# Output projection by token halves, with four weights kept in the large slots, and the second half's residual affine moved into the down projection

## The chip, the cores and the metric

The kernel runs on one core of a Trainium2 chip. The engines named below are TensorE (PE, with its weight loads, PEld), VectorE (DVE), ScalarE (ACT), GpSimd (POOL) and SyncE (SP), whose queue issues the DMA transfers. Each engine works through its own queue in order. The metric is the device time of one execution in microseconds (us).

## The reference

One layer of a diffusion backbone over 1024 tokens of width 1024. The attention part runs unchanged here; what matters begins with the output projection `w_out`, the first layer norm, and the convolutional feed-forward network.

```python
    y = (g_a * (o_a @ w_branch_a) + g_b * (o_b @ w_branch_b)) @ w_out
    x = _layer_norm(DEEPNORM_ALPHA * x + gate1 * y, ln1_g[l], ln1_b[l])
    h = x * (1.0 + scale2) + shift2
    y = _conv_ffn(h, w_up[l], conv_w[l], conv_b[l], w_down[l])
    x = _layer_norm(DEEPNORM_ALPHA * x + gate2 * y, ln2_g[l], ln2_b[l])

def _conv_ffn(h, w_up, conv_w, conv_b, w_down):
    u = h @ w_up                      # 1024 -> 5632
    u = depthwise_conv3_over_tokens(u, conv_w) + conv_b
    gate, val = jnp.split(u, 2, axis=-1)
    return (jax.nn.silu(gate) * val) @ w_down
```

Everything is float32. The kernel splits each operand into a high part that TensorE multiplies exactly and a low rest, so each product takes three matmuls (`mm3`: high by high, low by high, high by low).

## The kernel before

Features lie on the 128 partitions, so an activation of 1024 features is eight tiles, f = 0 to 7, of 128 x 1024 tokens. The stages that matter are, in the order in which PE meets them:

- `y`, the output projection. `wout_start(f)` loads the weights of the 128 output features of f, splits them (high part `hwo` by ACT, low part `lwo` by DVE) and loads the residual `x` into `z`; `wout_z` adds the gated product to `z` and gathers the sums `zs` and squares `zq` for the norm. Features 0 to 3 are computed for all 1024 tokens; then 4 to 7 for the token slices `LN1_S`: 0 to 511, 512 to 767 and 768 to 1023.
- LN1, made by `ln_steps` once for each slice: statistics by small matmuls (`sta`), the two diagonals (`dgr`, `dgm`), their broadcast over the partitions (`bcr`, `bcm`), and eight `apply` steps, which normalise a tile of `z` and call `emit1`. `emit1` makes `zo`, the affine value for the later residual (by POOL for odd f, by ACT for even f), and stores it in `zd`; makes the high part of the feed-forward input `B` and the modulated value over `z` itself (two ACT rows); and subtracts them for the low part of `B` (POOL for even f, DVE for odd f).
- `u`, three direct up tiles (two of gate, one of value, in slices; then three more at full width), whose operand is `B`.
- `up_tile` for j = 3 to 21: the up projection by a scheme of seven products instead of eight, into the banks a, b, c, d. Besides `B` it needs the operands `T13` and `T24`, sums of quarters of the modulated value, which `build` makes from `z` in four steps for each k = 0 to 3.
- The down projection: `ya`, first token half, 22 blocks j of 24 matmuls each, which need the weights `hwd`, `lwd` and the gated activation `g` (loaded back from `gd`); during block 6 the stored residuals are loaded from `zd` into the `zz` tiles. Then the second half, `yl`, and LN2.

From `y` on the order of PE's work is that of the code (`manual_schedule`); on the other engines a scheduler places the instructions. LN1 and `build` steps wait in the list `pend`. `tick` counts matmul columns, divided by 0.8, and releases the next step when the count reaches its number, so `LN1_F`, `LN1_D` and `BLD` place the steps between matmuls. Tiles come from pools: `ht` is a pool of large slots that `hput` gives back; the weights use two rings of four tiles, "w" and "wd".

Of the kernel before, what the change touches and what calls it, by code (L numbers as in the profile page):

```python
# [67 lines left out]
def layer_kernel(  # L68
# [773 lines left out]
    def weight(src, nm, n=8, tag="w", he=None, le=None, rtag="raw"):  # L842
        if rtag:
            r = post.tile([P, 8, P], F32, tag=rtag, name=f"r{nm}", bufs=3)[:, 0:n]
        else:
            r = ht(f"r{nm}", (P, n, P))
            hput(f"r{nm}")
        nc.sync.dma_start(r, src)
        pool = wq if tag == "w" else post
        h = pool.tile([P, 8, P], R32, tag=tag, name=f"h{nm}", bufs=4)[:, 0:n]  # L850
        l = pool.tile([P, 8, P], R32, tag=tag, name=f"l{nm}", bufs=4)[:, 0:n]
        split(r, h, l, he or nc.gpsimd, le or nc.gpsimd)
        return h, l
# [67 lines left out]
    def tiny(name):  # L921
        return post.tile([P, 8], F32, tag="tiny", name=name, bufs=6)
# [42 lines left out]
    def ln_steps(zs, zq, s, nm, emit, first, gap, gap1, gap2, each, pm=2, order=range(KT)):  # L965
        w = s.stop - s.start
        n = w // P
        mv, m2, rs, mr = (tiny(f"{a}{nm}") for a in ("mv", "m2", "rs", "mr"))
        bcs = []

        def stats():
            ln_flush()
            st = sml(f"st{nm}")
            for t in range(n):
# [32 lines left out]
    zs, zq = tm("zs1"), tm("zq1")  # L1007
    def wout_z(f, s, ps):
# [4 lines left out]
    for f in range(SPLIT_F):  # L1013
        if f > 1:
            wout_start(f)
        ps = big(f"y{f}")
        gemm(ps, wts[f], mrg, 8)
        for hf in (0, 1):
            wout_z(f, hsl(hf), ps[:, hsl(hf)])
    for f in range(SPLIT_F, KT):  # L1020
        wout_start(f)
    tp = {}

    def affine(o, f, src):
        nc.scalar.activation(o, src, AF.Identity, bias=lnx[:, 8 + f:9 + f], scale=lnx[:, f:f + 1])

    def sub(e, o, a, b, op=ALU.subtract):
        e.tensor_tensor(out=o, in0=a, in1=b, op=op)  # L1028

    def emit1(f, s):  # L1030
        hf = s.start // HALF
        w = s.stop - s.start
        c = slice(s.start - hf * HALF, s.stop - hf * HALF)
        if c.start == 0:
            tp["B", f, hf] = ht(f"B{f}_{hf}", (P, 2, HALF), R32)
        t = tp["B", f, hf]
        z = zv(f, s)
        o = ht(f"zo{f}_{s.start}", (P, w))
        hput(f"zo{f}_{s.start}")
        if f % 2:  # L1040
            nc.gpsimd.tensor_scalar(out=o, in0=z, scalar1=lnx[:, 16 + f:17 + f], scalar2=lnx[:, 24 + f:25 + f],
                                    op0=ALU.mult, op1=ALU.add)
        else:
            nc.scalar.activation(o, z, AF.Identity, bias=lnx[:, 24 + f:25 + f], scale=lnx[:, 16 + f:17 + f])
        nc.sync.dma_start(zd[f][:, s], o)
        affine(t[:, 0, c], f, z)
        affine(z, f, z)
        sub(nc.vector if f % 2 else nc.gpsimd, t[:, 1, c], z, t[:, 0, c].bitcast(F32))

    def build(k):  # L1050
        (b11, b21), (b12, b22) = [[zt_[k, hf][:, a] for a in (0, 1)] for hf in (0, 1)]
        st = {}
# [12 lines left out]
        def s2():  # L1065
            st["24"] = t = tm(f"t24_{k}").rearrange("p (a q) -> p a q", a=2)
            sub(nc.vector, t[:, 1], b22, st["13"][:, 1])
            sub(nc.gpsimd if k % 2 else nc.vector, t[:, 0], b21, t[:, 1])
            hput(f"z{k}_0", f"z{k}_1")

# [13 lines left out]

    hput(*[f"m{a}{f}" for f in range(KT) for a in "hl"])
# [12 lines left out]

    gr = {}
    npair = [0]  # L1100

    def gsplit(j, hf, t):
        r = tm(f"rg{j}_{hf}", w=HALF)
        nc.sync.dma_start(r, gd[j][:, hsl(hf)])
        split(r, t[:, 0], t[:, 1], nc.scalar, nc.vector)

    def ring(name, shape, dt=R32):
        pool, tag = ((wq, "w"), (post, "wd"))[npair[0] % 2]
        npair[0] += 1
        return pool.tile(list(shape), dt, tag=tag, name=name, bufs=4)  # L1110

    def wring(src, nm, n=8, le=None):
        r = post.tile([P, 8, P], F32, tag="raw", name=f"r{nm}", bufs=3)[:, 0:n]
        nc.sync.dma_start(r, src)
        h, l = ring(f"h{nm}", (P, 8, P))[:, 0:n], ring(f"l{nm}", (P, 8, P))[:, 0:n]
        split(r, h, l, nc.scalar, le or (nc.gpsimd if npair[0] % 4 else nc.vector))
        return h, l

# [40 lines left out]
    def up_conv(j):  # L1159
# [150 lines left out]
    for j in range(NF):  # L1310
# [3 lines left out]
        for f in range(KT):  # L1314
            mm3(acc[f], (w[0][:, f], w[1][:, f]), (g[:, 0], g[:, 1]), j == 0, j == NF - 1)
        gkeep(j)
        if j == 6:
            lnr = ht("lnr", (P, 2, HALF)), ht("lnr2", (P, 2, HALF))
            for a in (0, 1):
                nc.sync.dma_start(lnr[a], ln2_row[a].partition_broadcast(P))  # L1320
            for k in range(4):
                for hf in (0, 1):
                    zt_[k, hf] = ht(f"zz{k}_{hf}", (P, 2, HALF))
                    for a in (0, 1):
                        nc.sync.dma_start(zt_[k, hf][:, a], zd[k + 4 * a][:, hsl(hf)])

    zs2, zq2 = tm("zs2"), tm("zq2")
    for f in range(KT):
# [204 lines left out]
```

## Time and profile before

| what | value |
|---|---|
| median of three runs | 1653.31 us (1652.52 to 1653.62) |
| the profiled execution | 1654.61 us, its span 1652.8 us |
| mean granted PE clock | 0.985 |
| PE, DVE, POOL, ACT busy | 95%, 70%, 53%, 49% of the span |
| `y` | 830.5 to 923.2 us |
| `u` | 923.2 to 1019.8 us |
| product form of the up tiles | 1019.8 to 1388.6 us |
| `ya` | 1388.6 to 1508.4 us |

All starts are counted from the start of the span. PE is the busiest engine by far, so the profile is read for the stretches in which PE waits, and in these for the engine that it waits for and what that engine was doing.

### The profile page before, as it was taken

What the parts mean: (1) busy time and instruction counts of PE and PEld (TensorE: products, weight loads), DVE (VectorE), ACT (ScalarE), POOL (GpSimd) and SP (SyncE); (2) the same over time, 40 slices, a digit from 0 to 9 for tenths busy, and PEclk for the clock granted to TensorE, in tenths of its full rate; (3) what the DMA queues carried; (4) which work ended last, traced back from release to release, by engine and by line L of the source; (5) the groups of instructions that cost most, each with busy time, mean ns of one, the idle gap of its engine ahead of it and who ended that gap; (6) DMA issues with size and microseconds to landing.
All of it is one profiled execution on the core that took longest, in us unless ns stands there. A gap on an engine that the chain in (4) does not pass through costs nothing. (4 is left out here: it accounts for less than half of the span.)

```text
span 1652.8 us, 22324 instructions
## 1 busy us (share of the span) xinstructions
PE 1569.0 (95%) x7944; PEld 1302.9 (79%) x7944; DVE 1161.6 (70%) x1674; ACT 808.0 (49%) x1462; POOL 876.2 (53%) x781
## 2 busy tenths in 40 slices
PE   7999899999999999999999779999999999999996
PEld 5877788888877887777788667888888888888896
DVE  6899615538887777797644876789899997345535
ACT  4321222458887666787221663444544444433333
POOL 0673202426665555655324663566667773337885
PEclk9999899999999999999999889999999999999998
DMA  9688432322230111011521221122222228653453
GB/s 374 222 307 310 162 103 76 123 74 62 62 99 21 45 33 45 24 27 51 203 77 39 93 86 65 64 79 88 89 78 77 77 93 287 231 195 93 146 173 109
DMA packets 86800, 192.52 MB, mean 116 GB/s; under 512 B 11040, under 2 KB 25888, under 8 KB 86688
## 3 DMA queue, kind: packets, MB, share of 16 engines
q1 hardware_dynamic: 82080, 182.70, 33.3%
q10 hardware_dynamic: 4608, 8.39, 1.4%
q8 instruction: 62, 1.02, 0.3%
q14 instruction: 50, 0.41, 0.1%
HBM read 154.28 MB, written 28.38 MB: 111 GB/s over the span
## 5 line engine op out<-in xcount | busy, mean ns | idle before, releaser
L533 ACT CAST pth<-ptr 128x512 fp32r<-128x512 f32 x188 | 106.1, 591 | 62.4 <-PE ptr L524 59.9
L524 PE MATMUL ptr<-ident,p 128*128 128x128 f32 x816 | 130.0, 278 | 6.6 <-DVE ptl L534 4.6
L534 DVE TENSOR_TENSOR ptl<-ptr,pth 128x512 fp32r<-128x512 f32 x188 | 123.3, 683 | 16.6 <-ACT pth L533 15.6
L420 ACT ACTIVATE p<-p,nm 128x1024 f32<-128x1024 f32 (+2 forms) x128 | 125.4, 983 | 5.4 <-DVE p L453 5.1
L524 PEld LDWEIGHTS ptr<-ident,p 128*128 128x128 f32 x816 | 94.5, 140 | 37.2 <-DVE ptl L534 9.8
L85 POOL TENSOR_TENSOR wlg<-wg,whg 128x512 fp32r<-128x512 f32 x32 | 47.1, 1478 | 118.7 <-ACT whg L80 118.7
L545 PE MATMUL av<-pth,VT 128*128 128x512 f32 x236 | 106.2, 450 | 0.7 <-ACT avs L551 0.3
L546 PE MATMUL av<-ptl,VT 128*128 128x512 f32 x236 | 98.0, 415 | 5.2 <-POOL ptl L85 5.1
L90 PE MATMUL g<-hh,wlg 128*128 128x512 f32 x256 | 99.8, 390 | 0.4 <-POOL wlg L85 0.4
L88 PE MATMUL g<-hh,whg 128*128 128x512 f32 x256 | 100.0, 391 | 0.0
L89 PE MATMUL g<-hl,whg 128*128 128x512 f32 x256 | 99.7, 389 | 0.0
L453 DVE TENSOR_SCALAR_CACHE_REDUCE p<-s,cvt,nmc 128x1024 f32<-128x1024 f32 x64 | 84.4, 1340 | 11.4 <-PE s L409 7.9
L85 POOL TENSOR_TENSOR lwf<-rwf,hwf 128x1024 fp32r<-128x1024 f32 (+1 forms) x36 | 81.7, 2273 | 13.5 <-ACT hwf L80 12.6
L88 PE MATMUL yl<-gr,hwf 128*128 128x256 f32 (+1 forms) x264 | 85.4, 324 | 0.0
L90 PE MATMUL yl<-gr,lwf 128*128 128x256 f32 (+1 forms) x264 | 84.2, 319 | 0.0
L89 PE MATMUL yl<-gr,hwf 128*128 128x256 f32 (+1 forms) x264 | 84.1, 319 | 0.0
L85 POOL TENSOR_TENSOR lwd<-rwd,hwd 128x1024 fp32r<-128x1024 f32 x16 | 38.7, 2421 | 75.0 <-ACT hwd L80 66.1
L408 PE MATMUL s<-KL,q 128*128 128x512 f32 (+2 forms) x192 | 76.6, 399 | 1.7 <-DVE p L453 1.2
L82 POOL TENSOR_SCALAR pth<-prw 128x512 fp32r<-128x512 f32 x48 | 29.8, 620 | 89.5 <-ACT prw L530 85.2
L409 PE MATMUL s<-KL,q 128*128 128x512 f32 (+2 forms) x192 | 71.7, 373 | 0.0
L1233 POOL TENSOR_TENSOR uv<-ve,pe 128x512 f32<-128x512 f32 x19 | 30.4, 1603 | 73.7 <-DVE ve L1233 48.4
L80 ACT CAST wS<-s 128x512 fp32r<-128x512 f32 x76 | 44.6, 621 | 49.4 <-POOL s L1028 37.2
(382 smaller groups left out, 5313.5 us busy)
## 6 DMA issues: line engine op xcount, KB each, us to landing
wml<-in_wmodT_dram SPq DMA_DIRECT2D x48, 512.0 KB
ru<-in_w_up_dram SPq DMA_DIRECT2D x38, 512.0 KB
rwf<-in_w_dnf_dram SPq DMA_DIRECT2D x24, 512.0 KB
rg<-gd SPq DMA_DIRECT2D x44, 256.0 KB
rwd<-in_w_dn_dram SPq DMA_DIRECT2D x22, 512.0 KB
gd<-tg SPq DMA_DIRECT2D x19, 512.0 KB
wm<-in_wmodT_dram SPq DMA_DIRECT2D x16, 512.0 KB
wg<-in_w_g_dram SPq DMA_DIRECT2D x32, 256.0 KB
```

What stands on the lines that cost most here:

```text
L85: lo_eng.tensor_tensor(out=lo, in0=src, in1=hi.bitcast(F32), op=ALU.subtract)
L88: nc.tensor.matmul(ps, a[0], b[0], start=start, stop=False, skip_group_check=resumed)
L89: nc.tensor.matmul(ps, a[0], b[1], start=False, stop=False, skip_group_check=resumed)
L90: nc.tensor.matmul(ps, a[1], b[0], start=False, stop=stop, skip_group_check=resumed)
L408: nc.tensor.matmul(o, self.q[0][:, hs], ks, start=True, stop=False)
L420: nc.scalar.activation(p, s, AF.Exp, bias=nm[:, h:h + 1], scale=scale, accum_out=sm[:, h:h + 1])
L453: nc.vector.tensor_scalar(out=p, in0=o, scalar1=self.qscale(nqs)[:, hs] if self.br else -1.0, scalar2=self.other[:, hs], op0=ALU.mult, op1 ...
L524: nc.tensor.transpose(tr[:, h * P:(h + 1) * P], self.pslice(h, n), ident)
L533: nc.scalar.copy(hi, tr)
L534: nc.vector.tensor_tensor(out=lo, in0=tr, in1=hi.bitcast(F32), op=ALU.subtract)
L545: nc.tensor.matmul(self.av, v, hi, start=first, stop=False)
L546: nc.tensor.matmul(self.av, v, lo, start=False, stop=self.left == 0)
```

## The change

1. `y` is computed two features at a time (`y_pair`): first all eight features for tokens 0 to 511, then all eight for the second half, f = 4 to 7 there in its two slices. LN1 of the first half goes into `pend` before the second half's matmuls begin.
2. To have the weights for both passes, those of f = 0 to 3 (high and low, eight tiles) are kept in large slots of `ht`; 4 and 5 use the ring "w", 6 and 7 the ring "wd". The weights of the first up tile are loaded as soon as 4 and 5 are done, those of the second after `y`.
3. In the second token half `emit1` stores the normalised value as it is, without `zo`. The modulated value, which would overwrite it, goes into new tiles `v`, and `build` reads `v`. The affine left out is done later by `residual`, eight ACT rows of 128x512 on the loaded `zz` tiles, which the code puts into `pend` at block 12 of the down projection; `tick` is called there, and `drain` after it.
4. The additions to `zq` are all on DVE (before, POOL had those of f below 4). `LN1_F`, `LN1_D` have other numbers, `BLD` is 2400 instead of 3600.

PE has as many instructions of each shape as before.

```diff
-SPLIT_F = 4
-LN1_F = 6500.0, 2000.0, 2000.0
-LN1_D = 2500.0, 2000.0, 1000.0, 700.0
+LN1_F = 3500.0, 2000.0, 2000.0
+LN1_D = (2500.0, 2000.0, 2000.0, 2500.0), (2500.0, 2000.0, 1000.0, 700.0), (2500.0, 2000.0, 1000.0, 700.0)
-BLD = 3600.0
+BLD = 2400.0
+ZAJ = 12
+ZAF = 4500.0
...
     def wout_start(f, rtag="raw"):
-        wts[f] = weight(w_out[f], f"wo{f}", 8, tag="w" if f < SPLIT_F + 2 else "wd", he=nc.scalar, le=nc.vector,
-                        rtag=rtag)
+        wts[f] = weight(w_out[f], f"wo{f}", 8, tag=None if f < 4 else "wd" if f & 2 else "w", he=nc.scalar,
+                        le=nc.vector, rtag=rtag)
...
-        ln_add(zv(f, s), zs, zq, s, f == 0, f"a{f}_{s.start}", nc.vector if f >= SPLIT_F else nc.gpsimd, nc.gpsimd)
+        ln_add(zv(f, s), zs, zq, s, first, f"a{f}_{s.start}", nc.vector, nc.gpsimd)
...
+    def residual(o, f, src):
+        nc.scalar.activation(o, src, AF.Identity, bias=lnx[:, 24 + f:25 + f], scale=lnx[:, 16 + f:17 + f])
...
-        o = ht(f"zo{f}_{s.start}", (P, w))
-        hput(f"zo{f}_{s.start}")
-        if f % 2:
-            nc.gpsimd.tensor_scalar(out=o, in0=z, scalar1=lnx[:, 16 + f:17 + f], scalar2=lnx[:, 24 + f:25 + f],
-                                    op0=ALU.mult, op1=ALU.add)
+        v = z
+        if hf:
+            if f < 4 and c.start == 0:
+                tp["v", f] = ht(f"v{f}", (P, 2, HALF))
+            v = tp["v", f % 4][:, f // 4, c]
+            o = z
         else:
-            nc.scalar.activation(o, z, AF.Identity, bias=lnx[:, 24 + f:25 + f], scale=lnx[:, 16 + f:17 + f])
+            o = ht(f"zo{f}", (P, w))
+            hput(f"zo{f}")
+            if f % 2:
+                nc.gpsimd.tensor_scalar(out=o, in0=z, scalar1=lnx[:, 16 + f:17 + f], scalar2=lnx[:, 24 + f:25 + f],
+                                        op0=ALU.mult, op1=ALU.add)
+            else:
+                residual(o, f, z)
         nc.sync.dma_start(zd[f][:, s], o)
         affine(t[:, 0, c], f, z)
-        affine(z, f, z)
-        sub(nc.vector if f % 2 else nc.gpsimd, t[:, 1, c], z, t[:, 0, c].bitcast(F32))
+        affine(v, f, z)
+        sub(nc.vector if f % 2 else nc.gpsimd, t[:, 1, c], v, t[:, 0, c].bitcast(F32))
...
-    for si, s in enumerate(LN1_S):
-        w = s.stop - s.start
-        for f in range(SPLIT_F, KT, 2):
-            ps = big(f"y{f}_{si}")
-            for a in (0, 1):
-                mm_ticked(ps[:, a * HALF:a * HALF + w], wts[f + a], mrg, s)
-            for a in (0, 1):
-                wout_z(f + a, s, ps[:, a * HALF:a * HALF + w])
-        pend += ln_steps(zs, zq, s, f"a{si}", emit1, LN1_F[si], *LN1_D, order=(0, 4, 1, 5, 2, 6, 3, 7))
+    for f in range(0, KT, 2):
+        if f + 2 < KT:
+            for a in (2, 3):
+                wout_start(f + a)
+        y_pair(f, hsl(0), f == 0)
+    pend += ln1(0)
+    for f in (0, 2):
+        y_pair(f, hsl(1), f == 0)
+        hput(*[f"{a}wo{f + n}" for n in (0, 1) for a in "hl"])
+    for f in (4, 6):
+        for si in (1, 2):
+            y_pair(f, LN1_S[si])
+            if f == 6:
+                pend += ln1(si)
+        if f == 4:
+            up_weights(0, 0, 0)
+            up_weights(0, 1, 0)
...
+            tick(HALF / 0.8)
         gkeep(j)
+        if j == ZAJ:
+            pend += [(ZAF, lambda f=f: residual(zv(f, hsl(1)), f, zv(f, hsl(1)))) for f in range(KT)]
```

Three places show what becomes of it on the engines. In these rows the numbers behind an underscore tell buffers apart, and the operand's first digit is left out (`z_1` is the second token half of a `z` tile, `t_1` the `t13` or `t24` of k = 1).

On POOL, LN1 of the last quarter, 768 to 1023. Before:

```order
L1001 TENSOR_TENSOR z_1_9010<-z_1_9010,mba_9993 128x256
L1041 TENSOR_SCALAR zo_768_10037<-z_1_9010,lnx 128x256
L1001 TENSOR_TENSOR z_1_9010<-z_1_9010,mba_9993 128x256
L1041 TENSOR_SCALAR zo_768_10051<-z_1_9010,lnx 128x256
L1028 TENSOR_TENSOR B_1_9851<-z_1_8932,B_1_9851 128x256
L1001 TENSOR_TENSOR z_1_9217<-z_1_9217,mba_9993 128x256
L1041 TENSOR_SCALAR zo_768_10096<-z_1_9217,lnx 128x256
L1001 TENSOR_TENSOR z_1_9217<-z_1_9217,mba_9993 128x256
L1041 TENSOR_SCALAR zo_768_10110<-z_1_9217,lnx 128x256
L1028 TENSOR_TENSOR B_1_9863<-z_1_8932,B_1_9863 128x256
L1028 TENSOR_TENSOR t_0_10243<-z_1_8932 128x512
L1028 TENSOR_TENSOR t_1_10340<-z_1_9010 128x512
```

The next rows before are another `t_1` and the last two `B`. After, the same place:

```order
L1006 TENSOR_TENSOR z_1_9010<-z_1_9010,mba_9981 128x256 x2
L1027 TENSOR_TENSOR B_1_9844<-v_9845,B_1_9844 128x256
L1027 TENSOR_TENSOR B_1_9855<-v_9845,B_1_9855 128x256
L1027 TENSOR_TENSOR t_0_10209<-v_9845 128x512
L1006 TENSOR_TENSOR z_1_9047<-z_1_9047,mba_9981 128x256 x2
L1027 TENSOR_TENSOR t_1_10282<-v_9866 128x512
L1027 TENSOR_TENSOR B_1_9889<-v_9890,B_1_9889 128x256
L1027 TENSOR_TENSOR B_1_9900<-v_9890,B_1_9900 128x256
```

The four `zo` are gone, and one `t_1` that stood ahead of the last two `B` comes behind them.

On DVE, around the first tile in product form (`c_2` are the convolved halves of the last direct tile, `T24l`, `T13l` the low parts of the operands for k = 3). Before:

```order
L1134 SCALAR_TENSOR_TENSOR c_2_10422<-u_2_10356,cvt,c_2_10422 128x1023
L1138 TENSOR_TENSOR c_2_10352<-c_2_10352,c_2_10422 128x1024
L1028 TENSOR_TENSOR T24l_10454<-t_3_10446,T24h_10453 128x1024
L1028 TENSOR_TENSOR T13l_10450<-t_3_10443,T13h_10449 128x1024
L85 TENSOR_TENSOR wS_4_10606<-s_4_10553,wS_4_10606 128x512
```

After:

```order
L1165 SCALAR_TENSOR_TENSOR c_2_10408<-u_2_10345,cvt,c_2_10408 128x1023
L86 TENSOR_TENSOR wA_4_10545<-ru_4_10521,wA_4_10545 128x512
L1165 SCALAR_TENSOR_TENSOR c_2_10408<-u_2_10345,cvt,c_2_10408 128x1023
L1169 TENSOR_TENSOR c_2_10335<-c_2_10335,c_2_10408 128x1024
L1027 TENSOR_TENSOR T24l_10426<-t_3_10418,T24h_10425 128x1024
L86 TENSOR_TENSOR wS_4_10578<-s_4_10525,wS_4_10578 128x512
```

`T13l` of k = 3 has moved 16 rows up, and `T24l` is now the operand that takes the place of the `c` tile: it waits for the DMA that stores the product `c_2` in `gd2`, as `T13l` did before.

On ACT, at the start of the down projection (`hwd`, `g` and `gr` are casts for its blocks; the numbers of `hwd` and `g` rise with the block). Before:

```order
L80 CAST hwd_13240<-rwd_13238 128x1024
L80 CAST g_13204<-rg_0_13205 128x512
L1131 ACTIVATE tg_13066<-ug_13064,cvt 128x1024
L80 CAST g_13244<-rg_0_13245 128x512
L1131 ACTIVATE tv_13067<-uv_13065,cvt 128x1024
L1260 ACTIVATE tg_13066<-tg_13066 128x1024
L80 CAST gr_13313<-rg_1_13314 128x512
L80 CAST gr_13353<-rg_1_13354 128x512
L80 CAST hwd_13280<-rwd_13278 128x1024
L80 CAST g_13284<-rg_0_13285 128x512
```

After, from the third row on (the rows ahead of it are one residual between the same `hwd` and `g`):

```order
L1162 ACTIVATE tg_13038<-ug_13036,cvt 128x1024
L1024 ACTIVATE zz_1_13457<-zz_1_13457,lnx 128x512
L81 CAST g_13216<-rg_0_13217 128x512
L1024 ACTIVATE zz_1_13463<-zz_1_13463,lnx 128x512
L1162 ACTIVATE tv_13039<-uv_13037,cvt 128x1024
L1295 ACTIVATE tg_13038<-tg_13038 128x1024
L81 CAST gr_13285<-rg_1_13286 128x512
L1024 ACTIVATE zz_1_13463<-zz_1_13463,lnx 128x512
L1024 ACTIVATE zz_1_13469<-zz_1_13469,lnx 128x512
L81 CAST gr_13325<-rg_1_13326 128x512
L1024 ACTIVATE zz_1_13469<-zz_1_13469,lnx 128x512
L81 CAST hwd_13252<-rwd_13250 128x1024
```

Though the code adds them at block 12, the scheduler puts the eight residuals among the casts of the first five blocks, each behind the load of its `zz` tile.

More of the change, by code (lines that the diff above doesn't have):

```diff
@@ L1083, in mm_ticked, with ring, wring @@
             tick((s.stop - s.start) / 0.8)
-    hput(*[f"m{a}{f}" for f in range(KT) for a in "hl"])
+    npair = [0]
+    upw = {}
+    def ring(name, shape, dt=R32, which=None):
+        pool, tag = ((wq, "w"), (post, "wd"))[npair[0] % 2 if which is None else which]
+        npair[0] += which is None
+        return pool.tile(list(shape), dt, tag=tag, name=name, bufs=4)
+    def wring(src, nm, n=8, le=None, which=None):
+        r = post.tile([P, 8, P], F32, tag="raw", name=f"r{nm}", bufs=3)[:, 0:n]
+        nc.sync.dma_start(r, src)
+        h, l = (ring(f"{a}{nm}", (P, 8, P), which=which)[:, 0:n] for a in "hl")
+        split(r, h, l, nc.scalar, le or (nc.gpsimd if npair[0] % 4 else nc.vector))
+        return h, l
@@ new lines, in up_weights, with y_pair, ln1 @@
+    def up_weights(j, gv, which=None):
+        upw[j, gv] = wring(w_up[2 * j + gv], f"wu{gv}_{j}", le=nc.vector, which=which)
+    def y_pair(f, s, first=False):
+        w = s.stop - s.start
+        ps = big(f"y{f}_{s.start}_{w}")
+        for a in (0, 1):
+            mm_ticked(ps[:, a * HALF:a * HALF + w], wts[f + a], mrg, s)
+        for a in (0, 1):
+            wout_z(f + a, s, ps[:, a * HALF:a * HALF + w], first and a == 0)
+    def ln1(si):
+        return ln_steps(zs, zq, LN1_S[si], f"a{si}", emit1, LN1_F[si], *LN1_D[si], order=(0, 4, 1, 5, 2, 6, 3, 7))
@@ L1099, in layer_kernel @@
+    pend += ln1(0)
[10 more added lines that the diff above has]
+            up_weights(0, 1, 0)
+    hput(*[f"m{a}{f}" for f in range(KT) for a in "hl"])
     gr = {}
-    npair = [0]
     def gsplit(j, hf, t):
```

48 lines of the change are left out of this document (20 added, 28 removed).

## The prediction

> **What bounds the kernel now.** I read the totals first: PE is busy 95% of the span, so time can only be won where PE stands still or runs slowly. Then I looked for such places with the table by stretches of 10 us.
>
> ```profile
> PE 1569.0 (95%) x7944; PEld 1302.9 (79%) x7944; DVE 1161.6 (70%) x1674; ACT 808.0 (49%) x1462; POOL 876.2 (53%) x781
> ```
> ```profile
> 920.00:930.00 10.00, 6.14 (x36) 4.60 (x34) 9.97 (x12) 7.63 (x12) 9.81 (x8) 0.85 0.20 75
> 930.00:940.00 10.00, 4.10 (x9) 2.79 (x10) 5.83 (x9) 4.93 (x7) 7.98 (x8) 0.50 0.48 157
> 970.00:980.00 10.00, 2.56 (x12) 2.56 (x13) 6.56 (x5) 4.03 (x5) 9.89 (x9) 0.57 0.16 52
> 1020.00:1030.00 10.00, 5.88 (x24) 4.31 (x24) 6.56 (x5) 4.09 (x6) 5.77 (x5) 0.97 0.28 102
> sum 210.00, PE 184.72 PEld 156.92 DVE 130.28 ACT 89.31 POOL 102.96; mean PE 8.80 PEld 7.47 DVE 6.20 ACT 4.25 POOL 4.90
> ```
> The columns are the stretch, its length, then busy time and count for PE, weight loads, DVE, ACT and POOL, the granted clock and the DMA share. From 830 to 1040 PE is idle 210.00 - 184.72 = 25.3 us, and the clock falls to 0.50 and 0.57 behind the two long pauses. The waits of PE in the same window say on whom:
>
> ```profile
> PE u L89 <- POOL B L1028: 16.5, 3, 8.7
> PE b L88 <- ACT T24h L1057: 3.4, 1, 3.4
> PE u L90 <- DVE lwu L85: 1.7, 1, 1.7
> ```
> The direct up tiles `u` wait for the low halves of the normalised operand `B`, which POOL makes at the end of LN1: once for the first half (7.1 us) and once for the last quarter (8.7 us). The first tile in product form waits for its last operand, `T24`.
>
> How much is lost is read from the PE's timeline (start, duration):
>
> ```profile
> 923.07 0.28 PE L90 MATMUL y<-mh,lwo 128*128 128x256 f32 x1
> 923.19 0.39 PE L88 MATMUL u<-B,hwu 128*128 128x512 f32 x1
> 935.67 0.80 PE L89 MATMUL u<-B,hwu 128*128 128x512 f32 x1 [7.14 <-POOL B L1028]
> 977.44 0.58 PE L89 MATMUL u<-B,hwu 128*128 128x256 f32 x1 [8.70 <-POOL B L1028]
> 1019.83 0.39 PE L88 MATMUL a<-B,wA 128*128 128x512 f32 x1
> 1028.12 0.51 PE L88 MATMUL b<-T24h,wS 128*128 128x512 f32 x1 [3.37 <-ACT T24h L1057]
> 1029.38 0.79 PE L89 MATMUL b<-T24l,wS 128*128 128x512 f32 x1 [0.75 <-DVE T24l L1028]
> 1034.04 0.39 PE L90 MATMUL d<-T13h,wS 128*128 128x512 f32 x1
> 1034.27 0.39 PE L88 MATMUL c<-T13h,wS 128*128 128x512 f32 x1
> ```
> Undisturbed, a 512-column matmul follows the last after 0.2265 us (1034.04 to 1034.27) and a 256-column one after 0.12 us (923.07 to 923.19). `u` runs from 923.19 to 1019.83, 96.6 us, for 216 matmuls of 512 (48.9), 144 of 256 (17.4) and the last slices' small statistics and broadcast matmuls (2.5, my estimate from some ten of 0.25 us), 68.8 together: **27.8 us lost**. From 1019.83 to 1034.27, 14.4 us, stand 36 matmuls of 512 (8.15): **6.3 us lost**. These 34.1 us are the stake. That is 8.8 more than the idle time, since matmuls behind a pause run slowly: from 1029.38 to 1034.27 fourteen take 4.9 us where 3.2 would do.
>
> Here a page bears on it. The Trainium skill, TensorE: Matmul & The Clock Gate, Part 1, says that about 3.4 us of idleness halves the clock and that as much work restores it. By it each pause costs some 1.7 us (an estimate) on top of itself, also the one that I expect to remain; the 1.7 us just read agree, and the sum below would be 19.7 us instead of 20.3.
>
> **The change, part by part.** PE issues the same matmuls, so the time it works is unchanged; only waits move.
>
> *First half first.* All of `y` for tokens 0 to 511 now comes first, then LN1 of that half is released under 192 matmuls of 512 columns' worth of second-half `y` (44 us), where before 192 narrow ones (23 us) covered only its start. Its steps are spaced by 3500, 2500, 2000, 2000 and seven times 2500 units, 27500 in all; three matmuls of 512 columns (0.68 us) count 640, so it ends 29 us after 874, near 904, before `u` begins: the waits of 7.1 and 1.7 us at its start go. The up weights of the first tiles are loaded and split in that time as well. Inside `y` one thing becomes earlier: its first pair reaches k = 7 after 21 matmuls, not 42, so at 830.51 + 4.8 = 835.3, while the last merged operand is split on DVE behind other rows:
>
> ```profile
> 832.52 1.21 DVE L85 TENSOR_TENSOR lwo<-rwo,hwo 128x1024 fp32r<-128x1024 f32 x1
> 833.65 1.22 DVE L885 TENSOR_TENSOR bT<-bT,bT 128x1024 f32<-128x1024 f32 x1
> 835.98 1.23 DVE L85 TENSOR_TENSOR ml<-bT,mh 128x1024 fp32r<-128x1024 f32 x1 [1.11 <-ACT mh L80]
> ```
> The weight split at 832.52 now stands ahead of this, so `ml` ends near 836.0 and PE waits **0.5** (0 to 1.2). Each later weight is wanted after 5.4 us instead of 10.9; its split takes 1.2 us of DVE and 1.05 of ACT, which fits, and its load has some 4 us of slack.
>
> *Less POOL work in the second half.* The row that sets the 8.7 us wait is POOL's queue in the last quarter:
>
> ```profile
> 962.09 1.12 POOL L1041 TENSOR_SCALAR zo<-z,lnx 128x256 f32<-128x256 f32 x1
> 964.18 1.38 POOL L1041 TENSOR_SCALAR zo<-z,lnx 128x256 f32<-128x256 f32 x1
> 967.68 1.65 POOL L1041 TENSOR_SCALAR zo<-z,lnx 128x256 f32<-128x256 f32 x1
> 970.55 0.60 POOL L1041 TENSOR_SCALAR zo<-z,lnx 128x256 f32<-128x256 f32 x1
> 976.49 2.57 POOL L1028 TENSOR_TENSOR B<-z,B 128x256 fp32r<-128x256 f32 x2
> ```
> ```profile
> 959.31 0.37 ACT L994 COPY mba<-bcma 128x256 f32<-128x256 f32 x1
> ```
> The four `zo` are 4.75 us that go from each quarter. `t` for k = 0 and 1 still stands ahead of the last two `B`, the `t24` for k = 1 does not. From the copied broadcast to the last `B` (979.1) were 20 us; 4.75 and 2.3 less leave 12.5 to 13. The last quarter's statistics are now released without the first half's delay, its broadcast near 940.3, so the last `B` are there at 952 to 955, when PE, running from 923.7 without a pause, wants them at 952 and 955: **1.0** lost (0 to 10.7, the old wait with its slow clock).
>
> `u1_1` must take the PSUM of `u0_0`, which DVE frees with the second convolution step. The `T` steps now run ahead of it on DVE (BLD 2400 releases them earlier): 962.2 against 960.9, **1.3** (0 to 3).
>
> *T24 last.* The pause at `b` does not go. On DVE the operand `T13` of k = 3 moved up and `T24` of k = 3 took its place, in the tile that the DMA of `gd2` must first have left:
>
> ```profile
> 1024.71 2.23 DVE L1138 TENSOR_TENSOR c<-c,c 128x1024 f32<-128x1024 f32 x1
> 1028.10 1.22 DVE L1028 TENSOR_TENSOR T24l<-t,T24h 128x1024 fp32r<-128x1024 f32 x1 [1.17 <-ACT T24h L1057]
> 1031.29 1.23 DVE L1028 TENSOR_TENSOR T13l<-t,T13h 128x1024 fp32r<-128x1024 f32 x1 [1.96 <-DMA gd<-c]
> ```
> `T13` waited until 1031.29, 4.3 us after the product of the `c` tiles; `T24` then ends 12.7 us after the end of `u` (1032.52 - 1019.83). PE reaches it after 22 matmuls, 5.0 us: a wait of 7.7, in place of 4.1, and 1.1 to 1.7 of slow clock, so **8.8** lost against 6.3 (5 if the store lands at once, 11 at most).
>
> *The affine done later.* Eight ACTIVATE of 128x512 (0.6 us each, by the casts below) stand in ACT's queue between the casts that feed the first five `ya` blocks, each behind the load of its `zz` tile. PE has no gap in `ya` now, and blocks follow every 24 x 0.2265 = 5.43 us from 1388.57.
>
> ```profile
> 1389.00:1508.00 119.00, 119.00 (x526) 98.57 (x525) 51.66 (x57) 49.61 (x68) 42.70 (x19) 1.00 0.63 211
> ```
> ```profile
> 1388.57 0.39 PE L88 MATMUL ya<-g,hwd 128*128 128x512 f32 x1
> ```
> ```profile
> 1399.83 0.62 ACT L80 CAST gr<-rg 128x512 fp32r<-128x512 f32 x1 [6.07 <-DMA rg<-gd]
> 1400.36 1.05 ACT L80 CAST hwd<-rwd 128x1024 fp32r<-128x1024 f32 x1
> 1401.31 0.61 ACT L80 CAST g<-rg 128x512 fp32r<-128x512 f32 x1
> 1407.15 0.61 ACT L80 CAST g<-rg 128x512 fp32r<-128x512 f32 x1
> ```
> ```profile
> 1387.01 2.15 SPq L1325 DMA_DIRECT2D zz<-zd  x4
> 1394.51 0.32 SPq L1104 DMA_DIRECT2D rg<-gd  x1
> 1403.66 0.42 SPq L1325 DMA_DIRECT2D zz<-zd  x1
> ```
> The `rg` load issued at 1394.51 lets its cast start at 1399.83, 5.3 us later, with the queue full; I price the later `zz` loads at 4. The fourth block's `g`, cast at 1401.31, is wanted at 1404.86. The seventh residual ahead of it waits for a load that stands on SP behind an `rg` load, which waits for a split, whose cast ACT now makes later: issued near 1401.4, landed 1405.4, residual to 1406.0, `g` ready 1406.7, 1.8 late. The fifth's is wanted 5.43 us after that, at 1412.1, behind the last load, issued at 1403.66 before and near 1406.5 now: ready near 1412.4. I take **2.2** of new PE waits (0 to 6).
>
> The square sums of f below 4 go from POOL to DVE, six adds of 128x512 at about 0.7 us: DVE was busy 40 of 83 us there (840 to 923), which hides them.
>
> ```profile
> 840.00:923.00 83.00, 83.00 (x466) 72.44 (x465) 40.38 (x51) 24.83 (x36) 38.35 (x28) 1.00 0.14 48
> ```
> **Sum.** Lost after: 0.5 + 1.0 + 1.3 + 8.8 + 2.2 = 13.8; saved 34.1 - 13.8 = 20.3 us. The profiled execution took 1654.61 us, 1.3 above the median of 1653.31, so 1634.3 for it and **1633.0** as a median.
>
> **Rivals.**
> - *POOL remains late in the last quarter.* It is busy 9.89 of 10 us from 970 to 980 in the table above, and `t` steps could fill the room that `zo` leaves. Then 10.7 in place of 1.0: 1642.7. Against it: 7 us of 20 demonstrably leave the queue ahead of the last `B`.
> - *The weights of `y` come late.* The change relies on eight weights in 43 us. Were each from the third on 1 us late, 6 us more: 1639.0. Against it: PE had no gap in `y` at all, and the DMA share there was 0.14.
> - *Slower: the residuals serialise the down projection.* The loads of `rg4`, `rg5` and `rg6` wait on SP for splits whose casts now stand behind residuals, and later `zz` loads stand behind those on SP. If each of the eight residuals cost a full turn of load (5.3), residual and cast (1.2), 52 us pass where 23 are free (1387.3 to 1410.3): 29 us lost instead of 2.2, 1659.8. It decides the sign from (23 + 2.2 + 20.3) / 8 = 5.7 us a turn. Against it: SP issued four `zz` loads within 2.15 us, so they overlap.
> - *The change does not do what it says.* If the first half's LN1 were held up so far that `u` still waited for it at the start (27.8 less the 10.7 of the last quarter: 17.1), only 20.3 - 17.1 = 3.2 us were saved: 1650.1. Its release by ticks under 44 us of matmuls speaks against it.
>
> **How the numbers follow.** The forecast gets 0.60, POOL 0.17, the weights 0.06, LN1 held up 0.05, the slower case 0.12. The forecast's own range is 1625 (1653.3 less 34.1, plus 5 at `b` and 0.5 in `y`) to 1640 (the upper ends of the terms at `u1_1` and `b`, and 5 us in `ya`). Taking in POOL and the weights, and half of LN1's case, gives 1624 to 1648. A difference under 0.2% (3.3 us) is no difference that a measurement of this kernel tells. Faster 0.85; the same 0.04, from the edges of the last two cases; slower 0.11.
>
> **What would show it.** `u` starts without a pause near 924 and the products begin near 995; no `u` row waits for POOL's `B` longer than 2 us; PE's wait for `T24` at `b` grows to 6 to 9 us and follows a DMA of `gd`; in `ya` a wait of at most a few us for `g` in the fourth or fifth block, and ACT's residual rows idle for `zz`. I am wrong if POOL's `B` still holds `u` for 5 us or more, or if `ya` loses more than 5 us.

## Result: no difference

The changed kernel took 1651.8 us (median of 14 runs, 1647.75 to 1655.47) beside 1652.91 us for the kernel before (14 runs, 1649.82 to 1655.49): 0.9991 of the time before, 95% interval 0.9981 to 1.0. Some 20 us were forecast and about 1 came. The profiled execution has a span of 1651.9 us beside 1652.8.

The stages are read from the starts of the first PE rows of each. "Ahead" is all before `y`; "a to c" runs from the first product to the first one for bank c; "products" is the rest up to `ya`; "end" is `yl` and what follows. All in us, one profiled execution each (in the one of the kernel before, `yl` begins at 1508.2):

| kernel | ahead | `y` | `u` | a to c | products | `ya` | end | span |
|---|---|---|---|---|---|---|---|---|
| before | 830.5 | 92.7 | 96.6 | 14.4 | 354.3 | 119.7 | 144.6 | 1652.8 |
| after | 830.9 | 101.5 | 77.5 | 18.3 | 354.3 | 124.8 | 144.6 | 1651.9 |
| difference | +0.4 | +8.8 | -19.2 | +3.9 | 0.0 | +5.1 | 0.0 | -0.9 |

So 19.2 us were won in `u`, and 17.8 were given back in three places: `y`, the pause ahead of bank c, and `ya`.

### The profile page after: what moved, and what is told of

The parts are those of the page before. It is cut to its first block, busy times and chain, and to the rows that moved or that the text cites. A ratio compares the mean times of both kernels' runs of the same rounds, so it can differ in the third digit from the quotient of the medians.

```text
span 1651.9 us, 22300 instructions
## 1 busy us (share of the span) xinstructions
PE 1570.3 (95%) x7944; PEld 1304.5 (79%) x7944; DVE 1174.5 (71%) x1680; ACT 810.1 (49%) x1462; POOL 860.8 (52%) x767
## 5 line engine op out<-in xcount | busy, mean ns | idle before, releaser
L89 PE MATMUL ya<-g,hwd 128*128 128x512 f32 x176 | 69.4, 394 | 2.8 <-ACT g L81 2.1
```

The costliest lines, as they stand in the source:

```text
L89: nc.tensor.matmul(ps, a[0], b[0], start=start, stop=False, skip_group_check=resumed)
```

## The profile after

The totals, then the table by stretches of 10 us with the columns of the table shown of before (PE, weight loads, DVE, ACT, POOL, each busy time and count, then clock, DMA share, GB/s):

```profile
PE 1570.3 (95%) x7944; PEld 1304.5 (79%) x7944; DVE 1174.5 (71%) x1680; ACT 810.1 (49%) x1462; POOL 860.8 (52%) x767
```
```profile
890.00:900.00 10.00, 10.00 (x45) 8.27 (x45) 10.00 (x12) 6.81 (x10) 8.49 (x6) 1.00 0.08 29
900.00:910.00 10.00, 10.00 (x80) 9.77 (x80) 5.06 (x6) 5.01 (x8) 9.78 (x8) 1.00 0.35 131
960.00:970.00 10.00, 6.58 (x40) 6.17 (x40) 9.90 (x10) 6.16 (x8) 6.48 (x5) 0.83 0.05 15
970.00:980.00 10.00, 7.24 (x50) 6.56 (x49) 9.96 (x10) 7.61 (x8) 1.69 (x2) 1.00 0.00 0
830.00:1040.00 210.00, 190.04 (x978) 163.00 (x978) 138.65 (x167) 88.03 (x128) 92.40 (x77) 0.96 0.23 78
```
From 830 to 1040 PE now works 190.0 of 210 us, where it worked 184.7. POOL, which was full from 970 to 980, is nearly empty there (1.69); DVE is the full one (9.90 and 9.96 in the two stretches from 960 to 980). PE's waits in this window (engine, tile, line, whom it waits for; sum, times, longest):

```profile
PE b L90 <- DVE T24l L1027: 8.3, 1, 8.3
PE sta L981 <- POOL zs L948: 4.7, 1, 4.7
PE u L89 <- DVE c L1165: 2.8, 1, 2.8
PE u L90 <- DVE B L1027: 2.5, 1, 2.5
PE u L90 <- POOL B L1027: 0.9, 1, 0.9
PE y L90 <- DVE ml L86: 0.5, 1, 0.5
```
Of the two waits of `u` for POOL (16.5 us) 0.9 is left. Two new ones stand there, both for DVE, and one in `y` for the sums `zs` of the norm. They are followed back one at a time.

**In `y`.** The wait is that of the statistics matmuls `sta` of LN1 for tokens 512 to 767. The rows behind it, picked from the timeline (start, duration, instruction, and in brackets the idle time ahead of it and what ended that; some rows between them are left out), ACT's first, then DVE's, POOL's and PE's:

```profile
909.88 0.82 ACT L1024 ACTIVATE zo<-z,lnx 128x512 f32<-128x512 f32 x1 [2.94 <-DMA zd<-zo]
911.31 1.14 ACT L947 ACTIVATE sqa<-z 128x512 f32<-128x512 f32 x2
```
```profile
905.03 1.40 DVE L1014 SCALAR_TENSOR_TENSOR z<-y,modc,z 128x512 f32<-128x512 f32 x2
911.96 3.33 DVE L949 TENSOR_TENSOR zq<-zq,sqa 128x512 f32<-128x512 f32 x2 [5.53 <-ACT sqa L947]
916.41 0.86 DVE L1014 SCALAR_TENSOR_TENSOR z<-y,modc,z 128x256 f32<-128x256 f32 x2
918.85 1.21 DVE L86 TENSOR_TENSOR lwu<-rwu,hwu 128x1024 fp32r<-128x1024 f32 x1
919.99 0.86 DVE L1014 SCALAR_TENSOR_TENSOR z<-y,modc,z 128x256 f32<-128x256 f32 x2
920.77 1.58 DVE L86 TENSOR_TENSOR lwu<-rwu,hwu 128x1024 fp32r<-128x1024 f32 x1
923.66 0.87 DVE L1014 SCALAR_TENSOR_TENSOR z<-y,modc,z 128x256 f32<-128x256 f32 x2
```
```profile
897.12 2.24 POOL L1047 TENSOR_SCALAR zo<-z,lnx 128x512 f32<-128x512 f32 x1
924.22 1.59 POOL L948 TENSOR_TENSOR zs<-zs,z 128x256 f32<-128x256 f32 x2 [1.29 <-DVE z L1014]
```
```profile
925.86 0.58 PE L981 MATMUL sta<-onec,zs 128*128 128x1 f32 x2 [4.74 <-POOL zs L948]
```
ACT's `zo` for f = 6 waits until 909.88 for the DMA that stores an earlier `zo`. Behind it on ACT stand the squares `sqa` of the second half, ready to run since DVE's `z` at 905.03. DVE's additions `zq` wait for these, idle for 5.53 us, and the next three `z` rows of `y` (916.41, 919.99, 923.66) stand behind `zq`. POOL sums the last of them at 924.22, and PE gets it at 925.86. So LN1 of the first half, which the change put beside the second half's `y`, holds up that half's own sums through the queues of ACT and DVE. From 911.96 to the last `z` DVE idles for no more than 0.1 us, and in this stretch stand also the two splits `lwu` of the up weights (2.8 us), which the change brought forward too.

**In `u`.** DVE's rows in the last quarter, and the two PE rows that wait for them:

```profile
957.63 1.23 DVE L1027 TENSOR_TENSOR t<-v,z 128x512 f32<-128x512 f32 x1
959.65 1.78 DVE L1027 TENSOR_TENSOR t<-v,t 128x512 f32<-128x512 f32 x1
962.22 1.22 DVE L1027 TENSOR_TENSOR t<-z,t 128x512 f32<-128x512 f32 x1
963.36 0.68 DVE L1027 TENSOR_TENSOR t<-v,z 128x512 f32<-128x512 f32 x1
964.14 0.69 DVE L1027 TENSOR_TENSOR t<-v,t 128x512 f32<-128x512 f32 x1
964.75 1.83 DVE L1027 TENSOR_TENSOR B<-v,B 128x256 fp32r<-128x256 f32 x2
966.51 1.21 DVE L1027 TENSOR_TENSOR T13l<-t,T13h 128x1024 fp32r<-128x1024 f32 x1
...
968.78 2.31 DVE L1027 TENSOR_TENSOR T13l<-t,T13h 128x1024 fp32r<-128x1024 f32 x1
...
973.93 1.27 DVE L1163 SCALAR_TENSOR_TENSOR c<-u,cvt,c 128x1023 f32<-128x1023 f32 x1
...
975.72 1.27 DVE L1165 SCALAR_TENSOR_TENSOR c<-u,cvt,c 128x1023 f32<-128x1023 f32 x1
```
```profile
965.23 0.58 PE L90 MATMUL u<-B,hwu 128*128 128x256 f32 x1 [2.53 <-DVE B L1027]
977.14 0.47 PE L89 MATMUL u<-B,hwu 128*128 128x512 f32 x1 [2.76 <-DVE c L1165]
```
Five `t` rows, 5.6 us, stand among and ahead of the last two `B` low rows; the low parts of the `T` operands and four more `t` stand ahead of the second convolution step `c` (975.72), which frees the PSUM of the first direct tile.

**At b and in `ya`.** `T24l` for k = 3 still waits for the store of the `c` tile whose place it takes, and PE for it:

```profile
1022.10 1.23 DVE L1027 TENSOR_TENSOR T24l<-t,T24h 128x1024 fp32r<-128x1024 f32 x1 [4.47 <-DMA gd<-c]
```
```profile
1023.38 0.79 PE L90 MATMUL b<-T24l,wS 128*128 128x512 f32 x1 [8.34 <-DVE T24l L1027]
```
In `ya` ACT's residuals wait for their loads ahead of the cast of `g`:

```profile
1400.71 0.81 ACT L1024 ACTIVATE zz<-zz,lnx 128x512 f32<-128x512 f32 x1 [3.19 <-DMA zz<-zd]
1401.43 0.60 ACT L81 CAST g<-rg 128x512 fp32r<-128x512 f32 x1
```
```profile
1402.08 0.79 PE L89 MATMUL ya<-g,hwd 128*128 128x512 f32 x1 [2.07 <-ACT g L81]
```
With a wait of 0.74 for DVE in the first block and slow matmuls behind the pause (granted clock 0.83 from 1400 to 1410), this stage is 5.1 us longer.

## The experiments

The result left three losses to explain. For `y`: that the residual tiles `zo` of the first half cause it (their stores, their slots and their POOL and ACT rows), or that the split of the up weights on DVE does. For `u`: that DVE has too much to do of its own, or that the rows for the `T` operands stand ahead of what PE waits for. For `ya`: the residuals. The kernels e1 to e7 ran once each; f3 and f4 ran six and four times, and the profiled execution of f3 was the fastest of its six. Stage lengths are compared rather than single times, since the runs of one kernel spread over 8 us, and where the code is the same, the stage ahead of `y` came out anywhere from 826.5 to 831.0 us.

| kernel | ahead | `y` | `u` | a to c | `ya` | span |
|---|---|---|---|---|---|---|
| e1_no_residual | 831.0 | 103.9 | 80.3 | 15.9 | 119.7 | 1649.6 |
| e2_no_zo | 830.0 | 97.4 | 77.5 | 18.4 | 124.0 | 1646.2 |
| e2b_zo_unsaved | 828.9 | 98.5 | 79.1 | 16.4 | 124.8 | 1646.4 |
| e3_up_late | 826.5 | 101.2 | 77.5 | 18.3 | 124.7 | 1647.0 |
| e4_bld3600 | 828.5 | 101.5 | 77.4 | 15.4 | 124.1 | 1645.7 |
| e5_t24first | 829.4 | 102.7 | 77.5 | 14.2 | 124.3 | 1648.3 |
| e6_zo_kept | 829.3 | 102.9 | 78.8 | 16.8 | 119.7 | 1646.4 |
| e7_t_behind_c | 829.5 | 101.6 | 69.1 | 19.8 | 124.0 | 1643.1 |
| f3_res_t24_zoact | 827.0 | 95.7 | 79.1 | 12.5 | 119.7 | 1633.9 |
| f4_f3_t_behind_c | 828.8 | 97.2 | 69.1 | 16.0 | 119.7 | 1631.2 |

### Residuals left out

```diff
-            pend += [(ZAF, lambda f=f: residual(zv(f, hsl(1)), f, zv(f, hsl(1)))) for f in range(KT)]
+            pass
```

> The changed kernel without the eight residual rows on ACT (left out: the affine of the second half's residual, so the sum that enters LN2 lacks it). After the change ya takes 124.8 us from its first matmul to the first of yl; before it took 119.7. Theory (the residuals hold ACT's casts back): ya returns to 119.7 to 120.2 and PE waits there 0 to 0.5 us. Rival (the zz loads and the rg loads collide on the DMA queues whatever ACT does): ya stays at 123 to 125. The stages ahead of ya do not move by either: y 101.5, u 77.5, first product tile to c 18.3 us.

`ya` is back at 119.7 us and has no wait. So the eight residuals, placed among the first casts, cost all of the 5.1 us. `y` and `u` keep their waits (4.8, 2.7, 2.5), so the residuals have nothing to do with these. `u` is 2.9 us longer than after with the same waits, by a lower clock behind them (0.84 and 0.72 in the two stretches from 970 to 990, where it was 1.00): a stage behind a pause can't be read closer than that.

### The first half without `zo`

The high part of `B` is stored where `zo` was. Then `zo` computed as after, but the high part of `B` stored, so that its slot comes free at once.

```diff
-            o = ht(f"zo{f}", (P, w))
-            hput(f"zo{f}")
-            if f % 2:
...
-            else:
-                residual(o, f, z)
-        nc.sync.dma_start(zd[f][:, s], o)
+            o = t[:, 0, c].bitcast(F32)
         affine(t[:, 0, c], f, z)
+        nc.sync.dma_start(zd[f][:, s], o)
```

> The changed kernel with the first half's residual affine (zo, four rows on ACT and four on POOL) left out; the high part of B is stored in its place, so the same bytes go to zd. After the change y takes 101.5 us, of which PE waits 4.7 for zs at the second statistics. Theory A (squares of the second half stand behind zo rows on ACT, which wait for the stores of earlier zo) and theory B (POOL's own queue is full with zo rows) both say: this wait falls to 0 to 1 and y to 95 to 97.5. Theory C (the early split of the up weights on DVE holds the z rows back) says: it stays at 3.5 to 5.

```diff
-        nc.sync.dma_start(zd[f][:, s], o)
         affine(t[:, 0, c], f, z)
+        nc.sync.dma_start(zd[f][:, s], o if hf else t[:, 0, c].bitcast(F32))
```

> As the run without zo, but the eight zo rows are issued again and only their stores are left out (the high part of B is stored in their place). Theory A (the wait of a zo row for the store of an earlier one is what counts): the wait of 4.7 us for zs falls to 0 to 1.5, y to 95 to 98. Theory B (the zo rows' own time on POOL counts): it stays at 3 to 5, y at 100 to 102. Theory C: stays at 3.5 to 5.

PE's wait in `y`, first without `zo`, then with `zo` computed and not stored:

```profile
PE sta L981 <- POOL zs L948: 1.9, 1, 1.9
```
```profile
PE sta L981 <- POOL zs L948: 3.0, 1, 3.0
```
Of the 4.7 us, 1.7 come from waiting for the stores of `zo`, 1.1 from its rows, and 1.9 stay without it (the wait is 4.7 or 4.8 in all seven kernels that have these rows and stores as after). `y` is shorter by 4.1 and 3.0 us. The chain read from the trace is borne out for some 60% of the wait, less than was expected; the last 1.9 us and the slow matmuls behind them were not settled.

### The up weights later

```diff
-        if f == 4:
-            up_weights(0, 0, 0)
-            up_weights(0, 1, 0)
+    up_weights(0, 0, 0)
+    up_weights(0, 1, 0)
     hput(*[f"m{a}{f}" for f in range(KT) for a in "hl"])
```

> The changed kernel with the weights of the first up tile asked for after y, not after the fourth pair of it. Theory C (their split on DVE, two rows of 1.2 and 1.6 us, stands ahead of the z rows that the second statistics need): the wait for zs falls from 4.7 to 1.5 to 2.5 us. Theories A and B: it stays at 4 to 5. By all of them u may then wait for its weights, 0 to 4 us, at its start.

The wait stays at 4.8 us and `y` at 101.2. But this says nothing of the splits, because the edit did not move them: the code asks for the weights later, yet the scheduler puts DVE's rows in the same order as after:

```profile
913.99 1.21 DVE L86 TENSOR_TENSOR lwu<-rwu,hwu 128x1024 fp32r<-128x1024 f32 x1
915.12 0.86 DVE L1014 SCALAR_TENSOR_TENSOR z<-y,modc,z 128x256 f32<-128x256 f32 x2
915.91 1.58 DVE L86 TENSOR_TENSOR lwu<-rwu,hwu 128x1024 fp32r<-128x1024 f32 x1
918.79 0.87 DVE L1014 SCALAR_TENSOR_TENSOR z<-y,modc,z 128x256 f32<-128x256 f32 x2
```
So the splits remain a candidate. They push the last `z` row back by 2.6 us (an estimate: 918.85 to 919.99 and 920.77 to 922.27 in the rows of after), and they stand at the same place in the two kernels without the `zo` rows or their stores too. That would be enough for the 1.9 us left there, but no run took them away. The span of e3 is shorter only ahead of `y`, where nothing was changed.

### BLD as before

```diff
-BLD = 2400.0
+BLD = 3600.0
```

> The changed kernel with BLD back at 3600. In it T24h of k = 3 waits for the c tile's product and T13l of k = 3 for the store to gd2, as before the change. Theory (the operand order decides the pause at b): the stretch from the first product matmul to c falls from 18.3 to 14.0 to 15.5 us (14.4 before the change), and PE's wait there from 8.3 to 3.5 to 4.5. Rival (the early T steps only take the place of other DVE work, and the pause follows u's end whatever the order): 17.5 to 18.5. Theory for u: with the T steps later on DVE, the waits for B and for c in u (2.5 and 2.8 us) fall to under 1.5 each and u from 77.5 to 73 to 75.5; rival (they come from LN1's own rows): u stays at 77 to 78.

The waits of `u` are unchanged, 2.5 and 2.7 us. The `t` rows ahead of the last `B` and of that `c` stand in the same order as after, whatever `BLD` says, so the number can neither cause these waits nor cure them. What it does move are the operands of k = 3: at b the wait is for `T24h`, 4.1 us, and 0.5 for `T24l`, as before the change; the 15.4 us from a to c are only 0.5 below the least that kernels with the order of after gave there (15.9 to 18.4), so hardly a gain can be read from it.

### T24 ahead of T13 for k = 3

```diff
-        return [s1, s2, lambda: parts("13", nc.vector), lambda: parts("24", nc.vector)]
+        p13, p24 = lambda: parts("13", nc.vector), lambda: parts("24", nc.vector)
+        return [s1, s2, p24, p13] if k == 3 else [s1, s2, p13, p24]
```

> The changed kernel with BLD 2400, but for k = 3 the operand T24 is made ahead of T13, so that T13l is the one that waits for the store to gd2; PE needs it 12 matmuls (2.7 us) later. Theory (that store sets the pause): from the first product matmul to c 15 to 16.3 us in place of 18.3, the wait moves from b to d and is 5 to 6 us. Rival: 17.5 to 18.5 us.

```profile
PE d L90 <- DVE T13l L1027: 5.3, 1, 5.3
```
The pause goes from b to d, which stands 12 matmuls later (12 x 0.2265 = 2.7 us), and a to c takes 14.2 us. The wait for `T24l` at b was 8.3, 5.5, 8.0, 6.4, 8.1 and 6.2 us in the six kernels with the same order there (after, e1, e2, e2b, e3, e6): DVE's product of the `c` tiles took 2.2 us in after, e2 and e3 and 1.2 in the others, and the store behind it 2.7 to 4.5. 5.3 and 2.7 make 8.0, so the store was as late as after, and the 12 matmuls are the gain. The 14.2 us make it look larger, since with the pause at d some of the slow matmuls come behind the first one for c: from a to `ya` it is 369.9 us, beside 372.6 to 372.8 in after, e2 and e3. The same holds for a to c of f3 and f4 below.

### All eight `zo` of the second half kept, no residuals

Both halves treated as before the change, with the order of `y` of after.

```diff
-        if hf:
-            if f < 4 and c.start == 0:
-                tp["v", f] = ht(f"v{f}", (P, 2, HALF))
-            v = tp["v", f % 4][:, f // 4, c]
-            o = z
-        else:
-            o = ht(f"zo{f}", (P, w))
...
+        o = ht(f"zo{f}_{s.start}", (P, w))
+        hput(f"zo{f}_{s.start}")
...
-            pend += [(ZAF, lambda f=f: residual(zv(f, hsl(1)), f, zv(f, hsl(1)))) for f in range(KT)]
+            pass
```

> The changed kernel with its third part undone: zo and its store again in the second half as well, no v tiles, no residual rows; the order of y, the weights in large slots and the numbers stay. Theory: y stays at 101 to 104; POOL's four zo rows a quarter make u 4 to 9 us longer than 77.5; ya is 119.7 to 120.2. Rival (the zo rows of the second half cost nothing once LN1 of the first half is out of the way): u 77 to 79.

`u` takes 78.8 us, 1.3 more than after and far less than was expected. POOL's wait is back, without those for DVE's `B` and `c`:

```profile
PE u L90 <- POOL B L1027: 7.3, 1, 7.3
```
With `zo` PE waits 7.3 us for POOL; without, 0.9 for POOL and 5.3 for DVE. So the third part of the change, which costs 5.1 us in `ya`, is worth 1.3 us in `u` by these two executions, and that is less than the 2.9 us by which `u` differs with the same waits: another engine is late as soon as POOL is not. Nearly all that was won in `u` comes from the rest of the change, the new order of `y` with its weights and its spacing of LN1; these were not tried apart.

### The `t` rows held behind the convolution

`one` is a column of ones that is computed from the first convolved tile.

```diff
-            sub(nc.vector, t[:, 1], b12, b11)
+            nc.vector.scalar_tensor_tensor(out=t[:, 1], in0=b12, scalar=tp["one"], in1=b11, op0=ALU.mult,
+                                           op1=ALU.subtract)
...
             conv3(t, ups.pop((j, gv))[0], gv * NF + j)
+            if (j, gv) == (0, 0):
+                tp["one"] = post.tile([P, 1], F32, tag="one", name="one", bufs=1)
+                nc.vector.tensor_scalar(out=tp["one"], in0=t[:, 0:1], scalar1=0.0, scalar2=1.0, op0=ALU.mult,
+                                        op1=ALU.add)
```

> The first sums of the T operands (the rows t of k = 0 to 3 on DVE) are made as b12 * one - b11, with one a column that is computed from the first convolved tile c of direct tile 0 (always 1, so the values are the same). So no t row can stand ahead of the last B rows or of that c row. Theory: the waits of u for DVE's B (2.5 us) and for c (2.8 us) come from the t rows that the scheduler put ahead of them; then both fall, together by 3.5 to 5 us, and u becomes 72.5 to 74.5 us (77.5 in the changed kernel). The T operands come later, so the wait at b and d may grow: a to c 18 to 25 us. Rival: DVE is late there by its own LN1 rows; then the waits stay within 1 us of 2.5 and 2.8 and u stays 76.5 to 78.5.

`u` falls to 69.1 us, and in it PE waits for nothing. The longest wait in the window 820 to 1060, and DVE's rows where the five `t` stood:

```profile
PE b L90 <- DVE T24l L1027: 9.8, 1, 9.8
```
```profile
959.22 0.51 DVE L1027 TENSOR_TENSOR B<-v,B 128x256 fp32r<-128x256 f32 x1 [3.01 <-ACT v L1021]
960.20 0.42 DVE L1027 TENSOR_TENSOR B<-v,B 128x256 fp32r<-128x256 f32 x1 [0.47 <-ACT v L1021]
963.93 1.28 DVE L1164 SCALAR_TENSOR_TENSOR c<-u,cvt,c 128x1023 f32<-128x1023 f32 x1 [3.30 <-ACT c L1163]
```
The last `B` is done at 960.6, where it was 966.6 (1.4 us of this because `u` starts earlier), and DVE now idles between these rows: it was not short of time, its queue had the wrong order. The forecast of 72.5 to 74.5 us was too timid: it left out the wait of 0.9 us for POOL and the slow matmuls behind the waits (8.4 us less 6.2 us of waits). a to c grew by 1.5 us: the product of the `c` tiles, whose store `T24l` waits for, now ends 10.1 us behind `u`, and 7.7 in after.

### A version with the causes removed

All `zo` on ACT; T24 first for k = 3; and the residuals' scale and bias taken from a copy `rsc` that is derived from `gr` of block 12, so that their rows can't move ahead of it.

```diff
-            if f % 2:
-                nc.gpsimd.tensor_scalar(out=o, in0=z, scalar1=lnx[:, 16 + f:17 + f], scalar2=lnx[:, 24 + f:25 + f],
-                                        op0=ALU.mult, op1=ALU.add)
-            else:
-                residual(o, f, z)
+            residual(o, f, z)
...
-            pend += [(ZAF, lambda f=f: residual(zv(f, hsl(1)), f, zv(f, hsl(1)))) for f in range(KT)]
+            rsc = post.tile([P, 16], F32, tag="rsc", name="rsc", bufs=1)
+            nc.vector.scalar_tensor_tensor(out=rsc, in0=gr[j][:, 0, 0:16].bitcast(F32), scalar=0.0,
+                                           in1=lnx[:, 16:32], op0=ALU.mult, op1=ALU.add)
+            pend += [(ZAF, lambda f=f: nc.scalar.activation(zv(f, hsl(1)), zv(f, hsl(1)), AF.Identity,
+                                                            bias=rsc[:, 8 + f:9 + f], scale=rsc[:, f:f + 1]))
+                     for f in range(KT)]
```

> The changed kernel with three corrections: the residual rows take their scale from a copy that is made from block 12's operand, so they stand at blocks 12 and 13 in ACT's queue; T24 ahead of T13 for k = 3; the first half's zo all on ACT, where the squares of the second half now stand ahead of the zo row that waits for a store. Theory: ya 119.7 (-5.1), from the first product matmul to c 15 to 16.3 (-2.6), y 97 to 99.5 (-3), u 77.5 as it was: 9 to 12 us less than the change, ratio to the kernel before 0.992 to 0.995. Rival (each wait taken away comes back at the next place): ratio 0.997 to 1.000.

Six runs gave 1641.21 us in the median (1635.66 to 1643.19), 0.9922 of the time before (0.9907 to 0.9936; the kernel before beside them took 1653.79). `ya` has no wait; in `y` the wait is 1.8 us; the waits of `u` for `c` and `B` stay at 2.9 and 2.5. Then the same with the `t` rows held back:

> The same on top of f3. If the t rows are the cause, u falls from 79.1 to 73 to 76 us; with three operands for k = 3 late, a to c grows from 12.5 to 14 to 20. In all 3 us less to 3 us more than f3: 0.990 to 0.994 of the time before. If DVE's own rows are the cause, u stays at 78 to 80 and the time is 0.992 to 0.996.

Four runs gave 1634.47 us (1632.06 to 1637.06), 0.9886 of the time before (0.9861 to 0.9911): 19 us below the 1653.79 us of the kernel before beside them, and a little below the ratio of 0.990 to 0.994 that was expected. The longest wait that is left from 820 to 1060, and the first of the two groups of ACT's residual rows (the second follows at 1430.96), with PE waiting for nothing in `ya`:

```profile
PE d L90 <- DVE T13l L1027: 7.1, 1, 7.1
```
```profile
1426.14 2.93 ACT L1359 ACTIVATE zz<-zz,rsc 128x512 f32<-128x512 f32 x4 [1.63 <-DVE rsc L1357]
```
`u` fell by 10 us, more than was expected, and a to c grew by 3.5, as expected.

## Why the prediction was wrong

The undisturbed lengths that it worked with hold: `u` without waits takes 69.1 us (68.8 by its count of matmuls), `ya` 119.7, `y` 92.7. Against these, with 8.15 for a to c, after loses 8.8 + 8.4 + 10.1 + 5.1 = 32.4 us, where 0.5 + 2.3 + 8.8 + 2.2 = 13.8 were forecast.

- **First half first** (0.5 us in `y`; measured 8.8). This is the step that failed most. The merge stall was right, 0.53 us for `ml`, and so was that `u` would start without a wait. But LN1 was thought to run under the second half's matmuls at no cost, ending near 904; its last `B` came at 916.5, and its rows held up the squares and sums on which the next statistics wait. The splits of the up weights were put there at no cost as well. Room was judged by an average, for the square sums on DVE busy 40 of 83 us before, while the rows concerned fall in 890 to 926, with DVE at 10.0 of 10 in one stretch and POOL at 9.78 in the next. Whether the statistics matmuls of the next slice would have to wait was never asked. The experiments without `zo` show 2.8 us of the 4.7 us wait; the rest, for which the splits of the up weights are the likely cause by the order of DVE's rows, was not shown by a run and stays open.
- **Less POOL work, and `u1_1`** (1.0 and 1.3; measured 8.4 together). For POOL the step was right, 0.9 us of wait left, and the rival with POOL late did not come. It failed in pricing only POOL's queue for `B`. Half of the low parts come from DVE, whose queue had taken the `t` rows ahead of them. Holding these rows back took all of the 8.4 us away. For `u1_1` the wait was right, `T` steps ahead of the convolution, and the size was off: 2.8 us for 1.3. The reason given for it was not: with `BLD` back at 3600 the wait is the same (2.7).
- **T24 last** (8.8; measured 10.1). The mechanism holds, with the wait for the store of `gd` (8.3 for 7.7). The size differs by less than this wait varies between kernels that are alike there.
- **The affine done later** (2.2; measured 5.1). The mechanism holds, the seventh residual ahead of the `g` of the fourth block, 2.07 us for 1.8. Missing were a wait of 0.74 us for DVE in the first block and the slow clock behind the pause, together the larger half.
- **The rivals.** The weights of `y` were never waited for. LN1 held up did not delay the start of `u`, but what it delayed was close by. The residuals cost a wait or two, not a turn each. That the gain would be lost in `y` itself was no rival at all. Of the two signs of being wrong that were named, POOL's `B` did not hold `u` for long (0.9 us), and `ya` lost just over the 5 us named (5.1).

## To carry over

When work is moved under other matmuls, the question is not whether the engines have room on average there, but which rows of the covering stage now stand behind the moved ones in each queue, and which matmul waits for these. When one late engine is relieved, price the next engine's last row before the same matmul: here POOL's 7.3 us became 5.3 on DVE. And where a scheduler hoists rows as soon as their inputs are there, delays counted in the program do not hold them; a data dependency on the row that should go first does, and gave 8 us here. For the same reason an edit to the code proves something only once the rows have moved: the up weights asked for later were split at the same place.

## What the runs showed of the hardware

- **A short pause can halve the clock too, but need not.** In the last version PE pauses only 1.84 us ahead of the statistics, but these are eight matmuls of one column. By the table in stretches of 1 us the clock is 0.50 a little later, and the 27 `y` matmuls of 256 columns behind them take 4.8 us where 3.2 would do, as many as behind the pause of 4.74 us in after, and as in e2 behind one of 1.91:

```profile
924.00:925.00 1.00, 1.00 (x7) 1.00 (x6) 0.72 (x1) 0.00 (x0) 0.00 (x0) 0.50 0.00 0
```
  In f3 the same pause (1.82 us) ahead of the same eight matmuls left the clock at 1.00, and the 27 matmuls took 3.3 us:

```profile
921.00:922.00 1.00, 1.00 (x11) 1.00 (x9) 1.00 (x4) 0.00 (x0) 0.00 (x0) 1.00 0.00 0
```
  Before, the same eight matmuls without a pause left the clock at 1.00. The Trainium skill, TensorE: Matmul & The Clock Gate, Part 1, names an idle window of about 3.4 us; in f4 1.84 us idle and 1.0 us of nearly empty matmuls were enough. What decides between f3 and f4 no run here shows.
- **DVE and POOL rows stretch side by side, two- to threefold.** In the kernel after, POOL's `zo` of 128x512 took 2.24 and 2.12 us beside a busy DVE and 0.77 where DVE idled; DVE's `T13l` of 128x1024 took 1.21 us with POOL idle and 2.31 with POOL at work, and two `zq` of 128x512 3.33 us, though one took 0.68 in e2 (at 911.52), where POOL idled. So row times from a place where the other engine idles can't price a queue where both work. That the one slows the other is read from the coincidence and was not tried apart.
